# A bidirectional SSD in the gaps of a projection chain: heads in three staggered steps, masks in the exponents, one C B^T for both directions

## The chip, the core and the metric

The kernel runs on one core of one Trainium2 chip. The metric is the device time of one execution in microseconds. The engines are named as in the profile: PE (TensorE, with PEld its weight loads), DVE (VectorE), ACT (ScalarE), POOL (GpSimd), SP (SyncE, which issues most DMAs).

## The reference, cut to what matters

Two blocks of a model of width 2048 are computed in fp32. The first (attention, pooling, a convolutional feed-forward) and the last layer (neighbourhood attention) are not touched. Between them stands the even layer, on 16 meta tokens and 256 tokens (272 columns): projections, then a Mamba-2 SSD in both directions on 32 heads of 64 in 8 groups, a 31-tap convolution branch, and one output projection over both.

```python
z_a, xs, Bm, Cm, dt_f, dt_b, z_b, glu_v, glu_g = split_cols(rmsnorm(h) @ w_in)
xs, Bm, Cm = silu(depthwise_conv5([xs, Bm, Cm]))
# ssd_scan, one direction, chunks of 128:
A_cs = cumsum(log_a);  seg = A_cs[l] - A_cs[s]
Lmat = exp(where(s <= l, seg, -inf))        # per head
Y    = (C B^T * Lmat) @ (x * dt)            # C B^T per group of 4 heads
# y = forward + backward (flipped) + D * x
y_a = rmsnorm(y * silu(z_a))
y_b = silu(layernorm(conv31(glu_v * sigmoid(glu_g)))) * silu(z_b)
h   = h + [y_a, y_b] @ w_out
```

## The kernel before, in words

A projection (`project`) is 48 matmuls of 128x272 into one `acc` tile of PSUM: for each of 16 blocks of the contraction, weights high by input high (L226), high by low (L227) and low by high (L228). The weights arrive as `raw` chunks; ACT copies each half of a chunk to the rounded `wH` (L185), and POOL or DVE subtracts to get `wL` (L186). A table says which: of the chunks of B, C and xs POOL makes both halves, of the chunks of z_a, z_b and glu one, DVE the other. Three `acc` tiles, three `gp` tiles and two `cvp` tiles lie in PSUM.

The even layer goes through its projections in a fixed order: gates and values of the conv branch (glu, from about 1040 us), B and C with their 5-tap convolutions, xs, z_a (1470 to 1605 us), z_b (1608 to 1743 us), then the output projection `e_out`. Everything else is background work: `later(cost, fn)` puts a piece in a queue, and after each projection `run_bg(budget)` takes pieces until their costs reach the budget. The framework then orders the instructions of each engine by itself; engines run in order and wait for one another by semaphores.

The SSD is such background work. `group(g)` makes one C B^T for four heads: two matmuls into `gp` (L837), and a copy for each direction, masked by 0/1 constants, into an 800-wide `cb` (DVE L839, L841, L843, L844; ACT L840). `pair(hp)` treats two heads: transposes of x into `gp` (L866, copied out by L868), a DMA that spreads the cumulated decays over the partitions (`A4`), and per head `head`: five additions of a per-partition bias, limited at `EXP_MAX` (DVE L853), one exponential over 800 columns (ACT L855), one multiply by `cb` (DVE L856), and two additions on POOL that sum the directions where both are in force (L858). In a second step four matmuls with `e` as the weights' partner (L879) and three of the meta part (L885) go into a third `gp` tile, which DVE adds to x (L887). `meta_set` and `meta_x` do the 16 meta columns for eight heads at a time; `meta_x` makes four small copies `dupx` (DVE L820) into two buffers, each followed by a 32-row matmul (L822). In z_a and z_b one pair is done per projection or two.

```python
for a, b in ((144, 0), (672, 400)):
    nc.gpsimd.tensor_tensor(e[:, a:a + P], e[:, a:a + P], e[:, b:b + P], op=OP.add)
...
later(cost, g)
if held:
    later(*held.pop())
```

Of the kernel before, what the change touches and what calls it, by code (L numbers as in the profile page):

```python
# [15 lines left out]
P = 128  # L16
# [3 lines left out]
NM = 16  # L20
# [27 lines left out]
CC = {"mf": (0, 272), "mb": (272, 272), "m0f": (544, 272), "m0b": (816, 16), "bd": (832, 128)}  # L48
# [9 lines left out]
class Kernel:  # L58
# [14 lines left out]
    WIDE = 5  # L73
# [7 lines left out]
    def wide(self, n, name):  # L81
        return self.tp.tile([P, 800], F32, name=name, tag="wide", bufs=self.WIDE)[:, :n]
# [277 lines left out]
    def build(self):  # L360
# [6 lines left out]
        self.ph = lambda name: self.cp.tile([P, 960], F32, name=name, tag="phase", bufs=1)  # L367
# [8 lines left out]
    def load_x(self):  # L376
# [3 lines left out]
        for tag, size, n, steps in (("A4", 1088, 4, (2, 2)), ("A4", 1088, 4, (2, 2)), ("cb", 800, 3, (2, 1)),  # L380
                                    ("cb", 800, 3, (2, 1)), ("wide", 800, 2, (2,))):
# [259 lines left out]
    def even(self):  # L641
# [41 lines left out]
        def time_steps():  # L683
# [45 lines left out]
        for i in range(0, 16, 2):  # L729
            sig = []  # L730
            for j in (i, i + 1):
# [5 lines left out]
                self.run_bg(3.8)  # L737
                self.advance()
            for j in (i, i + 1):
# [5 lines left out]
                self.run_bg(3.8)  # L745
# [29 lines left out]
        for g in range(8):  # L775
            Bs.append(conv5(("B", g), 16 + g))
            self.run_bg(2.4)
            self.advance()
            Cs.append(conv5(("C", g), 24 + g))
            self.run_bg(2.4)  # L780
# [9 lines left out]
        def meta_set(t):  # L790

            a0 = self.wide(N + NM, "a0")
            z = self.wide(N + NM, "z0")
            for h in range(8):
                nc.sync.dma_start(a0[16 * h:16 * h + 16, :N], dA[8 * t + h:8 * t + h + 1].to_broadcast([NM, N]))
                nc.sync.dma_start(a0[16 * h:16 * h + 16, N:],
                                  dA[32 + 8 * t + h:32 + 8 * t + h + 1, :NM].to_broadcast([NM, NM]))
            nc.vector.tensor_scalar(z[:, :N], a0[:, :N], sb0[:, 0, t:t + 1], EXP_MAX, op0=OP.add, op1=OP.min)
            nc.vector.tensor_scalar(z[:, N:], a0[:, N:], sb0[:, 1, t:t + 1], EXP_MAX, op0=OP.add, op1=OP.min)
# [3 lines left out]
            dups = []  # L803
            for d in range(2):
                dup = self.tp.tile([P, 64], F32, name="dup", tag="dup", bufs=2)
                nc.vector.tensor_copy(dup.rearrange("p (a b) -> p a b", a=4),
                                      Bs[2 * t + d][:, :NM][:, None, :].to_broadcast([P, 4, NM]))
                dups.append(dup)
            yield
            ps = self.gp()[:, :N]  # L810
            for d in range(2):
                nc.tensor.matmul(ps[64 * d:64 * d + 64], dups[d], Cs[2 * t + d], start=True, stop=True)
            nc.vector.tensor_tensor(z[:, :N], ps, z[:, :N], op=OP.mult)
            W0[t] = self.split_act(z[:, :N], N)

        def meta_x(t):
            ps = self.gp()[:, :P]
# [5 lines left out]
            x0 = self.work("x0")  # L823
            nc.vector.tensor_tensor(x0[:, :P], ps, cols(cc, CC, "bd"), op=OP.mult)
# [3 lines left out]
            X0[t] = h, l  # L828

        def group(g):  # L830

            cb = self.tp.tile([P, 800], F32, name="cb", tag="cb", bufs=2)
            for c in range(2):
                ps = self.gp()[:, :N]
                nc.tensor.matmul(ps, Bs[g][:, NM + c * P:NM + (c + 1) * P], Cs[g], start=True, stop=True)  # L837
                if c == 0:
                    nc.vector.tensor_tensor(cb[:, :128], ps[:, NM:144], cols(cc, CC, "mb", P + NM, P), op=OP.mult)  # L839
                    nc.scalar.copy(cb[:, 128:144], ps[:, :NM])  # L840
                    nc.vector.tensor_tensor(cb[:, 144:400], ps[:, NM:], cols(cc, CC, "mf", 0, 256), op=OP.mult)  # L841
                else:
                    nc.vector.tensor_tensor(cb[:, 400:528], ps[:, 144:], cols(cc, CC, "mf", 0, P), op=OP.mult)  # L843
                    nc.vector.tensor_tensor(cb[:, 528:], ps, cols(cc, CC, "mb"), op=OP.mult)  # L844
# [407 lines left out]
```

## Time and profile before

| | |
|---|---|
| time, median of 3 runs (lowest to highest) | 2476.81 us (2475.53 to 2478.07) |
| the profiled execution: its own time | 2476.68 us |
| its span | 2474.8 us |
| PE busy | 2419.8 us (98%) |
| DVE busy | 1662.6 us (67%) |
| ACT busy | 1258.8 us (51%) |
| POOL busy | 1093.5 us (44%) |

The shares are means over the whole program. In the rows below, "A <- B" in a wait says whose result A waited for; in a group of instructions "out<-in" names the tiles. PEclk is the granted clock of TensorE, 1.00 being the higher of its two levels (2.4 GHz).

### The profile page before, as it was taken

What the parts mean: (1) busy time and instruction counts of PE and PEld (TensorE: products, weight loads), DVE (VectorE), ACT (ScalarE), POOL (GpSimd) and SP (SyncE); (2) the same over time, 40 slices, a digit from 0 to 9 for tenths busy, and PEclk for the clock granted to TensorE, in tenths of its full rate; (3) what the DMA queues carried; (4) which work ended last, traced back from release to release, by engine and by line L of the source; (5) the groups of instructions that cost most, each with busy time, mean ns of one, the idle gap of its engine ahead of it and who ended that gap; (6) DMA issues with size and microseconds to landing.
All of it is one profiled execution on the core that took longest, in us unless ns stands there. A gap on an engine that the chain in (4) does not pass through costs nothing. (4 is left out here: it accounts for less than half of the span.)

```text
span 2474.8 us, 48425 instructions
## 1 busy us (share of the span) xinstructions
PE 2419.8 (98%) x19742; PEld 2376.2 (96%) x19742; DVE 1662.6 (67%) x2897; ACT 1258.8 (51%) x1917; POOL 1093.5 (44%) x505
## 2 busy tenths in 40 slices
PE   8999999999999999999999998988999999999998
PEld 8998999999999999999999997878999999999998
DVE  6566466667666676889999979888767544444433
ACT  6564555554554554554445564744544444444553
POOL 1134444445445445644367855444334433333443
PEclk9999999999999999999999999999999999999999
DMA  8545655556656656864464554544666544445553
GB/s 283 186 140 190 231 193 186 187 177 219 233 176 216 226 181 215 256 216 174 149 206 169 188 199 140 194 154 153 218 234 207 187 161 164 171 171 171 194 187 120
DMA packets 116415, 471.62 MB, mean 191 GB/s; under 512 B 17376, under 2 KB 54496, under 8 KB 72416
## 3 DMA queue, kind: packets, MB, share of 16 engines
q1 hardware_dynamic: 94880, 443.87, 53.3%
q10 hardware_dynamic: 21312, 24.67, 2.8%
q8 instruction: 154, 2.52, 0.4%
q14 instruction: 69, 0.57, 0.1%
HBM read 448.94 MB, written 19.54 MB: 189 GB/s over the span
## 5 line engine op out<-in xcount | busy, mean ns | idle before, releaser
L226 PE MATMUL acc<-xh,wH 128*128 128x256 f32 (+1 forms) x5856 | 1676.2, 286 | 9.3 <-ACT xh L267 6.3
L228 PE MATMUL acc<-xh,wL 128*128 128x256 f32 (+1 forms) x5856 | 1668.3, 285 | 4.7 <-DVE wL L186 4.4
L227 PE MATMUL acc<-xl,wH 128*128 128x256 f32 (+1 forms) x5856 | 1670.6, 285 | 0.2 <-DVE xl L268 0.2
L186 POOL TENSOR_TENSOR wL<-raw,wH 128x1024 fp32r<-128x1024 f32 (+1 forms) x435 | 1041.0, 2395 | 1305.6 <-ACT wH L185 1187.6
L185 ACT ACTIVATE wH<-raw 128x1024 fp32r<-128x1024 f32 (+1 forms) x838 | 833.2, 998 | 867.2 <-PE acc L227 645.4
L226 PEld LDWEIGHTS acc<-xh,wH 128*128 128x128 f32 x5856 | 1108.8, 189 | 18.4 <-ACT xh L267 6.6
L228 PEld LDWEIGHTS acc<-xh,wL 128*128 128x128 f32 x5856 | 1108.2, 189 | 7.5 <-DVE wL L186 5.5
L227 PEld LDWEIGHTS acc<-xl,wH 128*128 128x128 f32 x5856 | 1108.4, 189 | 1.2 <-DVE xl L268 0.3
L186 DVE TENSOR_TENSOR wL<-raw,wH 128x1024 fp32r<-128x1024 f32 (+2 forms) x403 | 582.1, 1446 | 146.4 <-ACT wH L185 140.8
L666 DVE SCALAR_TENSOR_TENSOR cvp<-u,prm,cvp 128x264 f32<-128x264 f32 (+14 forms) x480 | 210.4, 487 | 0.7 <-ACT cvp L660 0.3
L265 DVE TENSOR_TENSOR xl<-y,xh 128x256 fp32r<-128x256 f32 x44 | 98.7, 2243 | 25.1 <-ACT xh L264 25.1
L239 PE MATMUL acc<-wH,xh 128*128 128x256 f32 x384 | 109.1, 286 | 5.9 <-ACT xh L267 5.9
L590 DVE TENSOR_TENSOR u<-acc,r 128x256 f32<-128x256 f32 x88 | 36.7, 418 | 111.2 <-PE acc L228 109.1
L241 PE MATMUL acc<-wH,xl 128*128 128x256 f32 x384 | 108.9, 285 | 0.7 <-DVE xl L268 0.7
L240 PE MATMUL acc<-wL,xh 128*128 128x256 f32 x384 | 107.7, 283 | 0.0
L239 PEld LDWEIGHTS acc<-wH,xh 128*128 128x128 f32 x384 | 72.9, 191 | 6.2 <-ACT xh L267 6.1
L291 DVE TENSOR_TENSOR nacc<-nacc,sq 128x272 f32<-128x272 f32 (+1 forms) x103 | 70.9, 688 | 9.6 <-ACT sq L280 8.7
L241 PEld LDWEIGHTS acc<-wH,xl 128*128 128x128 f32 x384 | 73.0, 190 | 1.8 <-DVE xl L268 1.4
L858 POOL TENSOR_TENSOR e<-e 128x128 f32<-128x128 f32 x64 | 48.9, 787 | 57.0 <-DVE e L856 56.1
L240 PEld LDWEIGHTS acc<-wL,xh 128*128 128x128 f32 x384 | 72.7, 190 | 0.1
L768 DVE SCALAR_TENSOR_TENSOR gp<-c,prm,gp 128x270 f32<-128x270 f32 (+1 forms) x128 | 63.7, 497 | 7.5 <-ACT gp L764 7.1
L853 DVE TENSOR_SCALAR e<-A,sbT 128x128 f32<-128x128 f32 (+3 forms) x160 | 65.1, 462 | 0.1
(229 smaller groups left out, 1396.5 us busy)
## 6 DMA issues: line engine op xcount, KB each, us to landing
raw<-in_e_w_in_dram SPq DMA_DIRECT2D x97, 1024.0 KB
raw<-in_w_up_dram SPq DMA_DIRECT2D x88, 1024.0 KB
raw<-in_o_w_in_dram SPq DMA_DIRECT2D x64, 1024.0 KB
raw<-in_w_down_dram SPq DMA_DIRECT2D x64, 704.0 KB
raw<-in_e_w_out_dram SPq DMA_DIRECT2D x32, 1024.0 KB
raw<-in_w_qkv_dram SPq DMA_DIRECT2D x21, 1024.0 KB
raw<-in_w_out_dram SPq DMA_DIRECT2D x16, 1024.0 KB
raw<-in_o_w_out_dram SPq DMA_DIRECT2D x16, 1024.0 KB
```

What stands on the lines that cost most here:

```text
L185: nc.scalar.activation(H[:, c], w[:, c], AF.Copy)
L186: eng.tensor_tensor(L[:, c], w[:, c], H[:, c].bitcast(F32), op=OP.subtract)
L226: nc.tensor.matmul(ps, wh, xh, start=k == 0, stop=False)
L227: nc.tensor.matmul(ps, wh, xl, start=False, stop=False)
L228: nc.tensor.matmul(ps, wl, xh, start=False, stop=k == n - 1)
L239: nc.tensor.matmul(ps[b], xh, H[:, o:o + 256], start=k == 0, stop=False)
L240: nc.tensor.matmul(ps[b], xh, L[:, o:o + 256], start=False, stop=False)
L241: nc.tensor.matmul(ps[b], xl, H[:, o:o + 256], start=False, stop=k == 15)
L265: nc.vector.tensor_tensor(l, x, h.bitcast(F32), op=OP.subtract)
L291: nc.vector.tensor_tensor(st["acc"], st["acc"], sq, op=OP.add)
L666: nc.vector.scalar_tensor_tensor(cps[i][:, a:b], u[i][:, a + s:b + s], self.prm_("dww", k * 16 + i), cps[i][:, a:b], op0=OP.mult, op1=OP.add)
L853: nc.vector.tensor_scalar(e[:, o:o + n], A4[:, d, i, l:l + n], sbT[:, c, 32 * d + h:32 * d + h + 1], EXP_MAX, op0=OP.add, op1=OP.min)
```

## The change

A pair becomes three steps, queued one projection slot apart: the transposes and the DMA of `A4`; the exponentials and their products (`heads`); the matmuls and the addition to x. The step of one pair is queued beside the other steps of its neighbours.

In `heads` the bias goes into the exponential itself: per head seven ACTIVATEs of 16 to 144 columns with the bias as a per-partition operand. The limit `EXP_MAX` is gone there; instead `cum` is held above -2^29, and on the triangular squares `A4` is held, by a minimum with constants of plus or minus 1e30 (`sq`), at or below -1e30 where the mask is zero. So the mask comes out of the exponential as zero. The squares of the backward direction go to a tile `eb`, DVE adds them (L865), and one multiply of 544 columns by a `cb` without masks (L866 of the new kernel) serves both directions. `group` is two plain copies on ACT. The result `py` goes into `cvp` instead of `gp`. `meta_set` takes in `meta_x`: the DMAs a step early, the copies `dup` and `dupx` into the tail of `z0` in the step before the matmuls, and one 128-column matmul for four. The tile `wide` shrinks from 800 to 544 columns, with seven buffers for five. The budgets are 3.4 for 3.8 (glu), 2.9 for 2.4 (B, C, xs), 3.9 for 4 (z_a, z_b); the pieces `yb` of z_b are split from the ninth z_b on, and the remaining queue is emptied beside the output projection with a budget of 3.9.

```diff
-                self.run_bg(3.8)
+                self.run_bg(3.4)
...
+            nc.vector.tensor_scalar(cum, cum, -2.0 ** 29, None, op0=OP.max)
...
-            self.run_bg(2.4)
+            self.run_bg(2.9)
...
+            dup = zt[:, 288:416].rearrange("p (d a b) -> p d a b", d=2, a=4)
+            for d in range(2):
+                nc.vector.tensor_copy(dup[:, d], Bs[2 * t + d][:, :NM][:, None, :].to_broadcast([P, 4, NM]))
+            dupx = zt[:, 416:].rearrange("p (i a b) -> p i a b", i=4, a=2)
+            for i in range(4):
+                nc.vector.tensor_copy(dupx[:, i], xs[4 * t + i][:, :NM][:, None, :].to_broadcast([P, 2, NM]))
...
+            yield
+            px = self.gp()[:, :P]
+            nc.tensor.matmul(px, zt[:, 416:], self.ident, start=True, stop=True)
...
-            for i in range(4):
-                dup = self.tp.tile([P, 32], F32, name="dupx", tag="dupx", bufs=2)
-                nc.vector.tensor_copy(dup.rearrange("p (a b) -> p a b", a=2),
-                                      xs[4 * t + i][:, :NM][:, None, :].to_broadcast([P, 2, NM]))
-                nc.tensor.matmul(ps[32 * i:32 * i + 32], dup, self.ident, start=True, stop=True)
...
-                if c == 0:
-                    nc.vector.tensor_tensor(cb[:, :128], ps[:, NM:144], cols(cc, CC, "mb", P + NM, P), op=OP.mult)
...
+                nc.scalar.copy(cb[:, N * (1 - c):N * (2 - c)], ps)
...
-            nc.scalar.activation(e, e, AF.Exp)
-            nc.vector.tensor_tensor(e, e, cb, op=OP.mult)
-            for a, b in ((144, 0), (672, 400)):
-                nc.gpsimd.tensor_tensor(e[:, a:a + P], e[:, a:a + P], e[:, b:b + P], op=OP.add)
...
+            def exp(to, i, d, c, l, n):
+                h = 32 * d + 2 * hp + i
+                nc.scalar.activation(to, A4[:, d, i, l:l + n], AF.Exp, bias=sbT[:, c, h:h + 1])
+
+            for i in range(2):
+                exp(E[i][:, 416:544], i, 0, 0, 144, P)
+                exp(E[i][:, 272:288], i, 1, 0, 0, NM)
+                exp(E[i][:, 0:144], i, 1, 1, 0, 144)
+            for d in range(2):
+                sq = A4[:, d, :, NM:].rearrange("p i (c l) -> p i c l", c=2)
+                nc.vector.tensor_tensor(sq, sq, cols(cc, CC, "sq", P * d, P)[:, None, None, :]
+                                        .to_broadcast([P, 2, 2, P]), op=OP.min)
+            for i in range(2):
+                for c in range(2):
+                    o = 288 - 144 * c
+                    exp(E[i][:, o:o + P], i, 0, c, NM + P * c, P)
+                    exp(B[i][:, 1 - c], i, 1, c, NM + P * c, P)
+            for e, eb in zip(E, B):
+                nc.vector.tensor_tensor(squares(e), squares(e), eb, op=OP.add)
+                nc.vector.tensor_tensor(e, e, CBF[hp // 2], op=OP.mult)
...
-            py = self.gp()[:, :N]
+            yield
+            E = heads(hp, A4)
+            yield
+            py = self.cvp()
...
+        for s in range(18):
+            if s >= 2:
+                later(1.0, pairs[s - 2])
+            if s % 4 == 1 and s < 16:
+                later(1.8, metas[s // 4])
+            if s < 16:
+                if s % 2 == 0:
+                    self.later(1.0, group, s // 2)
+                later(0.6, pairs[s])
+            if 1 <= s < 17:
+                later(3.6, pairs[s - 1])
...
+            self.run_bg(3.9)
+            if i >= 8:
+                ready(i - 8)
...
-            self.run_bg(1e9)
+            self.run_bg(3.9)
```

On PE, between the second and the third projection of z_b, stand the matmuls of one pair, a group's C B^T and the transposes of a later pair (the numbers tell tiles apart). Before:

```order
L879 MATMUL gp_19933<-e_19747,xt_19742 64x272
L879 MATMUL gp_19933<-e_19757,xt_19742 64x272
L879 MATMUL gp_19933<-e_19747,xt_19742 64x272
L879 MATMUL gp_19933<-e_19757,xt_19742 64x272
L885 MATMUL gp_19933<-xh_19836,x0_19660 128x272
L885 MATMUL gp_19933<-xl_19837,x0_19660 128x272
L885 MATMUL gp_19933<-xh_19836,x0_19661 128x272
L837 MATMUL gp_19943<-c5_16513,c5_16438 128x272
L837 MATMUL gp_19948<-c5_16513,c5_16438 128x272
L866 MATMUL gp_19952<-cst_73,c5_17652 128x128 x2
```

and now:

```order
L888 MATMUL cvp_19840<-e_19751,xt_19627 64x272
L888 MATMUL cvp_19840<-e_19752,xt_19627 64x272
L888 MATMUL cvp_19840<-e_19751,xt_19627 64x272
L888 MATMUL cvp_19840<-e_19752,xt_19627 64x272
L894 MATMUL cvp_19840<-xh_19739,x0_19735 128x272
L894 MATMUL cvp_19840<-xl_19740,x0_19735 128x272
L894 MATMUL cvp_19840<-xh_19739,x0_19736 128x272
L833 MATMUL gp_19850<-c5_16507,c5_16430 128x272
L833 MATMUL gp_19853<-c5_16507,c5_16430 128x272
L879 MATMUL gp_19859<-cst_73,c5_17674 128x128 x2
```

The pair's seven matmuls move from the pool of three `gp` tiles to `cvp`; four tiles of `gp` follow one another before, three now.

On ACT, about the same place. Before, from one copy of weights to the next tanh but one:

```order
L185 ACTIVATE wH_19986<-raw_19868 128x1024
L947 ACTIVATE tanh_19928<-z_b_19927 128x272
L840 COPY cb_19942<-gp_19943 128x16
L868 COPY xt_19955<-gp_19952 128x256
L855 ACTIVATE e_19970<-e_19970 128x800
L185 ACTIVATE wH_20084<-raw_19980 128x1024
L855 ACTIVATE e_20062<-e_20062 128x800
L185 ACTIVATE wH_20088<-raw_19980 128x1024
L947 ACTIVATE tanh_20040<-z_b_20039 128x272
```

and now, from a copy of weights to the next:

```order
L185 ACTIVATE wH_19894<-raw_19775 128x1024
L965 ACTIVATE tanh_19835<-z_b_19834 128x272
L849 ACTIVATE e_19988<-A4_19856,sbT_13204 128x128
L849 ACTIVATE e_19988<-A4_19856,sbT_13204 128x16
L834 COPY cb_19849<-gp_19850 128x272
L849 ACTIVATE e_19988<-A4_19856,sbT_13204 128x144
L834 COPY cb_19849<-gp_19853 128x272
L881 COPY xt_19862<-gp_19859 128x256
L849 ACTIVATE e_20176<-A4_19979,sbT_13204 128x128
L849 ACTIVATE e_20177<-A4_19979,sbT_13204 128x128
L849 ACTIVATE e_19987<-A4_19856,sbT_13204 128x128 x2
L849 ACTIVATE e_19988<-A4_19856,sbT_13204 128x128
L849 ACTIVATE eb_19989<-A4_19856,sbT_13204 128x128 x2
L185 ACTIVATE wH_20013<-raw_19888 128x1024
```

One exponential of 800 columns per head has become seven short ones, which read `A4` and no longer a tile that DVE has written, and the copies of C B^T are ACT's, 272 columns each.

On DVE, the copies of the second half of x's meta columns for the first eight heads. Before, behind the fourth z_a:

```order
L937 TENSOR_TENSOR z_a_18354<-acc_18305,r_13269 128x272
L820 COPY dupx_18365<-c5_17045 128x32
L820 COPY dupx_18368<-c5_17120 128x32
L839 TENSOR_TENSOR cb_18377<-gp_18378,cc_13200 128x128
L186 TENSOR_TENSOR wL_18422<-raw_18295,wH_18421 128x1024
L824 TENSOR_TENSOR x0_18371<-gp_18358,cc_13200 128x128
L841 TENSOR_TENSOR cb_18377<-gp_18378,cc_13200 128x256
```

and now, for the second eight heads, in the convolutions of the last xs (L770 is a tap of these):

```order
L801 TENSOR_SCALAR z0_18613<-z0_18613,sb0_13205 128x272
L770 SCALAR_TENSOR_TENSOR gp_17899<-c5_17897,prm_72,gp_17899 128x271
L802 TENSOR_SCALAR z0_18613<-z0_18613,sb0_13205 128x16
L770 SCALAR_TENSOR_TENSOR gp_17899<-c5_17897,prm_72,gp_17899 128x270
L806 COPY z0_18613<-c5_15958 128x64
L806 COPY z0_18613<-c5_16112 128x64
L809 COPY z0_18613<-c5_17206 128x32
L809 COPY z0_18613<-c5_17283 128x32
L809 COPY z0_18613<-c5_17360 128x32
L809 COPY z0_18613<-c5_17443 128x32
L764 TENSOR_TENSOR c5_17974<-acc_17925,r_13269 128x272
L186 TENSOR_TENSOR wL_17997<-raw_17915,wH_17996 128x1024
```

The copies stood right ahead of their matmuls; now all six of a set stand in a step before, with other work behind them.

## Rows read from the trace of the kernel before

**Rows 1.** The page's first line: the span.

```profile
span 2474.8 us, 48425 instructions
```

**Rows 2.** Windows; columns: stretch, its length, busy us (instructions) by engine, PEclk, DMA, GB/s.

```profile
1800.00:1900.00 100.00, 100.00 (x802) 99.92 (x801) 67.82 (x92) 46.30 (x65) 39.58 (x16) 1.00 0.67 220
1200.00:1300.00 100.00, 95.60 (x755) 94.45 (x754) 96.96 (x203) 46.73 (x58) 53.49 (x22) 1.00 0.52 174
1300.00:1400.00 100.00, 100.00 (x800) 99.79 (x799) 92.75 (x219) 57.27 (x81) 79.58 (x34) 1.00 0.52 178
1465.00:1745.00 280.00, 255.52 (x1842) 229.96 (x1841) 234.79 (x448) 153.01 (x227) 131.78 (x97) 0.95 0.51 166
1612.00:1711.00 99.00, 85.90 (x607) 75.29 (x607) 91.50 (x178) 46.45 (x74) 43.68 (x42) 0.93 0.49 154
1490.00:1500.00 10.00, 5.31 (x26) 4.18 (x27) 7.62 (x18) 2.56 (x8) 4.44 (x1) 0.66 0.57 206
1570.00:1580.00 10.00, 7.64 (x28) 5.05 (x27) 7.62 (x19) 9.93 (x15) 6.35 (x5) 0.67 0.45 153
1680.00:1690.00 10.00, 5.29 (x26) 5.29 (x27) 9.72 (x27) 4.91 (x8) 3.15 (x5) 0.66 0.56 181
```

**Rows 3.** Waits of PE, 1465 to 1745 us; columns: total us, times, longest.

```profile
PE gp L866 <- DVE c L887: 11.6, 2, 6.5
PE gp L822 <- DVE dupx L820: 5.4, 1, 5.4
PE gp L879 <- POOL e L858: 3.9, 2, 2.4
PE gp L885 <- DVE xl L265: 3.2, 1, 3.2
```

**Rows 4.** Waits of PE, 1200 to 1300 us.

```profile
PE acc L228 <- DVE wL L186: 4.4, 4, 1.7
```

**Rows 5.** The tile view of z_b, its first line.

```profile
L946 DVE SCALAR_TENSOR_TENSOR z_b<-acc,r x16: 422/429/442, 1612.3 to 1741.7; 128x272 f32<-128x272 f32 x16
```

**Rows 6.** Waits of the other engines, 1465 to 1745 us.

```profile
POOL e L858 <- DVE e L856: 56.1, 18, 6.8
...
ACT e L855 <- DVE e L853: 24.1, 8, 6.2
```

**Rows 7.** DVE by line and shape, 1465 to 1745 us.

```profile
L186 DVE TENSOR_TENSOR wL<-raw,wH 128x1024 fp32r<-128x1024 f32 x33 | 47.8, 1449 | 8.0 <-ACT wH L185 7.8
L856 DVE TENSOR_TENSOR e<-e,cb 128x800 f32<-128x800 f32 x32 | 36.8, 1170 | 3.1 <-ACT e L855 3.1
```

**Rows 8.** The page's costliest groups, whole span.

```profile
L666 DVE SCALAR_TENSOR_TENSOR cvp<-u,prm,cvp 128x264 f32<-128x264 f32 (+14 forms) x480 | 210.4, 487 | 0.7 <-ACT cvp L660 0.3
...
L858 POOL TENSOR_TENSOR e<-e 128x128 f32<-128x128 f32 x64 | 48.9, 787 | 57.0 <-DVE e L856 56.1
...
L853 DVE TENSOR_SCALAR e<-A,sbT 128x128 f32<-128x128 f32 (+3 forms) x160 | 65.1, 462 | 0.1
```

**Rows 9.** ACT by line and shape, 1612 to 1711 us.

```profile
L855 ACT ACTIVATE e<-e 128x800 f32<-128x800 f32 x15 | 13.0, 867 | 20.8 <-DVE e L853 20.8
...
L855 ACT ACT_TABLE_LOAD x1 | 1.3, 1283 | 1.5 <-DVE e L853 1.5
...
L868 ACT COPY xt<-gp 128x256 f32<-128x256 f32 x8 | 2.9, 364 | 3.2 <-PE gp L866 3.2
...
L826 ACT ACTIVATE x<-x 128x128 fp32r<-128x128 f32 x1 | 0.3, 310 | 3.7 <-DVE x L824 3.7
```

**Rows 10.** POOL by line and shape, 1760 to 1820 us.

```profile
L186 POOL TENSOR_TENSOR wL<-raw,wH 128x1024 fp32r<-128x1024 f32 x11 | 26.4, 2402 | 40.8 <-ACT wH L185 28.1 <-PE acc L227 12.7
```

**Rows 11.** DVE by line and shape, 1760 to 1820 us.

```profile
L291 DVE TENSOR_TENSOR nacc<-nacc,sq 128x272 f32<-128x272 f32 x11 | 26.7, 2428 | 8.7 <-ACT sq L280 8.7
```

**Rows 12.** ACT by line and shape, 100 to 200 us.

```profile
L475 ACT ACTIVATE s<-s,mx 128x128 f32<-128x128 f32 x8 | 3.2, 403 | 8.7 <-DVE mx L473 5.7 <-DVE win L514 2.9
```

**Rows 13.** PE by line and shape, 1465 to 1745 us.

```profile
L822 PE MATMUL gp<-cst,dupx 128*32 128x128 f32 x32 | 4.2, 302 | 5.4 <-DVE dupx L820 5.4
```

More of the change, by code (lines that the diff above doesn't have):

```diff
@@ L81, in wide @@
     def wide(self, n, name):
-        return self.tp.tile([P, 800], F32, name=name, tag="wide", bufs=self.WIDE)[:, :n]
+        return self.tp.tile([P, 544], F32, name=name, tag="wide", bufs=self.WIDE)[:, :n]
     def small(self, n, name):
@@ L828, in meta_x @@
             X0[t] = h, l
+            W0[t] = self.split_act(z[:, :N], N)
         def group(g):
-            cb = self.tp.tile([P, 800], F32, name="cb", tag="cb", bufs=2)
-            for c in range(2):
+            cb = self.tp.tile([P, 800], F32, name="cb", tag="cb", bufs=2)[:, :2 * N]
+            for c in (1, 0):
                 ps = self.gp()[:, :N]
                 nc.tensor.matmul(ps, Bs[g][:, NM + c * P:NM + (c + 1) * P], Cs[g], start=True, stop=True)
-                if c == 0:
-                    nc.vector.tensor_tensor(cb[:, :128], ps[:, NM:144], cols(cc, CC, "mb", P + NM, P), op=OP.mult)
[L840 to L844, printed above, removed]
@@ new lines, in group, with squares, heads @@
+            CBF[g] = cb
+        def squares(t):
+            return t[:, 144:432].rearrange("p (c n) -> p c n", n=144)[:, :, :P]
+        def heads(hp, A4):
+            E = [self.wide(544, "e") for i in range(2)]
+            B = [self.tp.tile([P, 2, P], F32, name="eb", tag="eb", bufs=2) for i in range(2)]
+            def exp(to, i, d, c, l, n):
[17 more added lines that the diff above has]
+                nc.vector.tensor_tensor(e, e, CBF[hp // 2], op=OP.mult)
+            return E
@@ L863, in pair @@
             x = xs[hp]
+            A4 = self.tp.tile([P, 2, 2, N], F32, name="A4", tag="A4", bufs=2)
+            for d in range(2):
+                nc.sync.dma_start(A4[:, d].rearrange("p a b -> p (a b)"),
+                                  dA[32 * d + 2 * hp:32 * d + 2 * hp + 2].rearrange("a b -> (a b)")[None, :]
+                                  .to_broadcast([P, 2 * N]))
             px = self.gp()
@@ L868, in pair @@
             nc.scalar.copy(xt, px[:, :256])
-            A4 = self.tp.tile([P, 2, 2, N], F32, name="A4", tag="A4", bufs=2)
-            for d in range(2):
-                nc.sync.dma_start(A4[:, d].rearrange("p a b -> p (a b)"),
-                                  dA[32 * d + 2 * hp:32 * d + 2 * hp + 2].rearrange("a b -> (a b)")[None, :]
-                                  .to_broadcast([P, 2 * N]))
-            E = [head(2 * hp, A4), head(2 * hp + 1, A4)]
             yield
-            py = self.gp()[:, :N]
+            E = heads(hp, A4)
+            yield
+            py = self.cvp()
             for c in range(2):
@@ L911, in even @@
         later = lambda cost, g: self.later(cost, next, g, None)
-        held = []
         cn = conformer_norm()
-        norms = [(2.8, cn)] * 4 + [(1.8, cn)] * 4
-        def start(cost, g, rest):
-            later(cost, g)
-            if held:
-                later(*held.pop())
-            held.append((rest, g))
-            if norms:
-                later(*norms.pop(0))
-        for t in range(4):
-            start(2.5, meta_set(t), 0.4)
-            self.later(1.0, meta_x, t)
-            for g in (2 * t, 2 * t + 1):
-                self.later(2.0, group, g)
-                for hp in (2 * g, 2 * g + 1):
-                    start(4.0, pair(hp), 0.5)
-        later(*held.pop())
+        norms = [2.8] * 4 + [1.8] * 4
+        pairs, metas = [pair(hp) for hp in range(16)], [meta_set(t) for t in range(4)]
+        later(0.1, metas[0])
+        later(3.4, metas[0])
+        for s in range(18):
[9 more added lines that the diff above has]
+                later(3.6, pairs[s - 1])
+            if s % 4 == 2 and s < 14:
+                later(0.1, metas[s // 4 + 1])
+            if s % 4 == 3 and s < 15:
+                later(3.4, metas[s // 4 + 1])
+            if norms:
+                later(norms.pop(0), cn)
         gates = []
@@ L949, in even @@
             nc.vector.scalar_tensor_tensor(conv[i], th, 1.0, conv[i], op0=OP.add, op1=OP.mult)
[L950 removed]
+            self.run_bg(3.9)
+            if i >= 8:
+                ready(i - 8)
         del X, self.X
[L952 to L955 removed]
+        for i in range(8, 16):
+            ready(i)
         st = self.norm_begin(N)
```

76 lines of the change are left out of this document (29 added, 47 removed).

## The prediction

> **What bounds the kernel now.** I take the sum against the profiled execution: 2476.7 us, of which 2474.8 is the span [rows 1]; the median of the runs shown is 2476.8, so one figure serves for both. I first read windows. From 1800 to 1900 us PE is never idle and does 802 matmuls in 100 us [rows 2]: 0.1247 us each, 5.99 for a projection of 48. That is the floor, and most of the program sits on it. Two stretches that the change touches don't: 1200 to 1300 (end of glu), where PE lacks 4.4 of 100 while DVE is busy for 97, and 1465 to 1745 (z_a and z_b), where PE lacks 24.5 of 280 and its clock is 0.95 [rows 2]. The convolutions between them keep PE busy all the time (1300 to 1400 us [rows 2]), so nothing is to be won there.
>
> Next the waits of PE. In z_a and z_b four causes carry it [rows 3]: transposes L866 wait for a free `gp` tile, because DVE's L887 has not yet emptied the one of the pair before (11.6 us in two waits); one 32-row matmul waits for its small copy (5.4); the pair's own matmuls wait for POOL's additions (3.9); the meta part waits for a rounded piece `xl` (3.2). 0.4 more falls on L837. In glu all 4.4 is PE waiting for `wL` of DVE [rows 4]. So DVE is late both times.
>
> Then z_b slot by slot. Its sixteen projections end in 129.4 us [rows 5]; the last five have no heads beside them and take 5.99 each, which leaves 99.4 for ten, 9.9 per slot. The window of those ten slots, 1612 to 1711, shows DVE busy for 91.5 of 99 us, ACT for 46.5, POOL for 43.7 [rows 2]. POOL waits 56.1 us for DVE's multiply, and ACT 24.1 us for DVE's additions [rows 6]: DVE is at the head of that chain. PE was busy for 85.9 there; without the two clock dips in it (below) that is 82.3, or 8.2 per slot. **The slot of 9.9 is DVE's, and the next limit is PE's own 8.2.**
>
> **What DVE loses and gets.** Per pair before: two multiplies of 1.17 [rows 7], ten additions with a limit, 65.1/16 = 4.07 [rows 8], and half of a group's four masked copies, up to 272 columns each, for which DVE's reading of `acc` in z_b shows 0.43 [rows 5], so up to 0.8. Together 7.2. After: per pair two minima of 512 columns, two additions of 256, two multiplies of 544. No row shows these widths; between 272 columns at 0.43 [rows 5] and 800 at 1.17 [rows 7] a straight line gives 0.77, 0.41 and 0.81, sum of the six 4.0. (The 1.17 contains blocked time, so the line is rather high.) So 3.2 less per pair. The window of ten slots holds the transposes of eight pairs [rows 9], 0.8 per slot, and DVE's 9.15 becomes 9.15 - 2.6 = 6.6. POOL loses its 64 additions, 48.9 us [rows 8].
>
> Two-input operations can be held up by POOL. While POOL split weights at 2.40 us each [rows 10], the 272-column addition L291 took 2.43 [rows 11], against 0.43 for the operation of that width that reads PSUM [rows 5]: 2.0 us lost to one split. In a slot with one split of POOL that makes 6.6 to 8.6 for DVE. The Trainium skill, "SBUF — State Buffer", section "Who interferes with whom", says that DVE and GpSimd share one port pair as an exclusive lock, and that a DVE instruction with two SBUF inputs fully blocks against a GpSimd instruction that reads SBUF. The trace agrees (2.43 beside 2.40), and the rule speaks against this change, since all six new operations have two SBUF inputs. If each slot lost a whole split, the slots would come to 8.6 on DVE, still below 9.9.
>
> **What ACT gets.** Per pair, minus two exponentials of 0.87 [rows 9]; plus twelve of 128 to 144 columns, between 0.31 (a copy of 128 columns with no bias [rows 9]) and 0.40 (an exponential of 128 with a per-partition bias [rows 12]), 3.7 to 4.8; plus two of 16 columns, 0.3; plus half of two copies of C B^T at about 0.37 each (L868, 256 columns, 0.36 [rows 9]). Net +2.7 to +3.8. ACT's 4.65 per slot becomes 7.4 to 8.5 where a whole pair falls in it. That is close to PE's 8.2.
>
> A new hand-over comes with it: the minimum overwrites `A4`, so DVE waits until ACT's first exponentials have read it, and ACT's other eight wait for the minimum. Behind the waiting DVE instruction stand the evictions of `acc` and `wL`; behind ACT's stand `wH` and the copies that free `gp`; PE waits for all of these. The order puts a weight copy or the other head between the two halves, so I price it at 0 to 1.0 per pair.
>
> **The terms.**
> (1) Glu. In the order, the taps from the time-step projection to the end of glu fall from 112 to 103, and one `wL` goes from DVE to POOL: about 9 times 0.44 (210.4/480 [rows 8]) and 1.45 [rows 7], 5.4 off DVE, more than the 4.4 it is late. -4.4 (0 to -4.4). The taps move on into the convolutions, but the budget of 2.9 changes little there: the order has about 8 taps per projection before and after, because it was the scheduler that decided.
> (2) Waits in z. The 5.4 go: the copies stand a step early, covered by convolution taps. The 12.0 on `gp` go: the pair's result is in `cvp`, which the convolutions have left, and `gp` is emptied by ACT. What is late next is ACT's copies behind up to 4.8 us of exponentials, hidden by the projection between; if that cover is gone, the 12 come back as waits for ACT. The 3.9 go with POOL's additions, since the products are queued a slot ahead of the matmuls. The 3.2 for `xl` stay; the first set is as tight as before. -21.3 (0 to -24.5).
> (3) Clock. Four windows of 10 us at 0.66 or 0.67, so part of each at the lower level, each with a wait that goes in it or just before: the first, the second and the last have 5.31, 7.64 and 5.29 us of busy PE [rows 2] and lose 1.8, 2.5 and 1.8, and the third, around 1635 us, is like the last. -8 (0 to -9.5 with small dips).
> (4) Twelve matmuls of 32 rows fewer: three quarters of 4.2 us [rows 13], less what overlaps. -2.5 (0 to -3.1).
> (5) New limit. PE's 8.2 per slot is met by ACT's 7.4 to 8.5 and DVE's 6.6 to 8.6 with a hand-over. Were none in the way it costs 0; with ACT at 8.5 plus a whole hand-over the slot is 9.5, +1.3 in each of 16, +21. I take 8.65, near the upper ends of both engines: +0.45 times 16, **+7**.
>
> At nothing: the DMAs of `A4` and `z0` a step earlier (same count; on SP they stand ahead of weight loads, and no wait of PE on a weight's DMA is in [rows 3]; DMA share 0.49 in z_b [rows 2]); the smaller `wide`, seven for five; the clamp of `cum`, one operation; the split of `yb` in z_b, which the order had there before; the budget beside the output projection, since the queue is empty by then in both orders.
>
> Sum: -4.4 - 21.3 - 8 - 2.5 + 7 = -29.2, so **2447.5 us**.
>
> **The rivals.**
> (A) ScalarE becomes the pace, and it gets slower. Exponentials, the tanh of z_b's gate and the square roots of norms are spread over ACT's order; if each pair slot saw two switches of its tables at 1.28 [rows 9], it would need 8.5 + 2.6 = 11.1 us. Then waits of PE for ACT replace all the old ones: 16 times 1.2 = +19, less terms 1 and 4, so about 2489. It decides from 9.9 + 6.9/16 = 10.3 us per slot. For it: the order has 51 table loads in the program, 43 before. Against it: in z_a and z_b they fall from 17 to 12, and the extra ones lie in the convolutions, where PE runs ahead. The Trainium skill, "ScalarE: Activation LUTs", section "What ACT_TABLE_LOAD costs", gives about 2.66 us per switch, the load and a drain. By that estimate two switches would be 5.3 us, and the slot 13.8. The trace shows the load's 1283 ns, and no run here shows a drain behind it. Chance 0.10.
> (B) DVE stays the pace: six two-input operations meet POOL's splits more than once per slot, 6.6 + 2.0 and more, and the hand-over keeps it at 9.9. Only glu and the fewer matmuls remain: 2470. For it speaks that DVE's multiplies take 1.17 [rows 7], already partly blocked; against it, that POOL's additions, which hold the same ports, are gone. Chance 0.12, half of it within 0.2%.
> (C) Half of the waits go: ACT now empties `gp` from behind its exponentials, or the matmuls wait for the products. -4.4 - 10.6 - 4 - 2.5 + 7 = -14.5, about 2462. Chance 0.16.
> The forecast itself, 2434 to 2456, has 0.62.
>
> **How the numbers follow.** 2447.5 is the likeliest case. The range of 2434 to 2470 goes from all waits and dips gone with no new limit (-40, and a little for dips between the windows) to (B); it leaves out (A) and the slow half of (B). A measurement here tells about 0.2%, 5 us, from no change. Faster by that: 0.62 + 0.16 + half of (B) = 0.84; the same: 0.06; slower: 0.10.
>
> **What would show it.** PE waits in z_a and z_b below 8 us instead of 24.5, none for L866 on L887 or for `dupx`; clock above 0.98 there; ten busy slots of z_b at 8.5 to 8.9; DVE below 85% and ACT above 75% busy in them; no wait for `wL` around 1240 us; no POOL addition of `e`. Wrong if PE waits for ACT's copies or exponentials (A, C), if DVE's new operations average well over 1 us (B), or if a wait appears in the convolutions, where three pairs' exponentials now start.

## The result, and the profile after

The changed kernel takes 2449.3 us (2448.7 to 2449.7, four runs) against 2477.1 us before: ratio 0.9889, 95% interval 0.9877 to 0.9901, 28 us less. The forecast was 2447.5. Its profiled execution took 2449.6 us.

Windows of the kernel after; columns as in [rows 2]. First the ten slots of z_b with heads, then z_a and z_b as a whole, the end of glu, and five windows with a lower clock:

```profile
1602.00:1683.00 81.00, 79.27 (x583) 70.75 (x582) 73.23 (x119) 57.88 (x149) 22.62 (x9) 0.98 0.50 166
1465.00:1717.00 252.00, 241.10 (x1784) 221.08 (x1783) 210.16 (x318) 178.87 (x391) 84.05 (x32) 0.97 0.54 182
1200.00:1300.00 100.00, 99.97 (x799) 99.75 (x798) 99.58 (x206) 48.48 (x62) 54.67 (x23) 1.00 0.53 183
1470.00:1480.00 10.00, 4.43 (x25) 3.04 (x24) 8.49 (x12) 5.00 (x9) 2.56 (x1) 0.93 0.55 194
1480.00:1490.00 10.00, 10.00 (x75) 10.00 (x75) 8.47 (x19) 4.94 (x11) 2.40 (x1) 0.90 0.42 149
1550.00:1560.00 10.00, 6.80 (x38) 5.16 (x37) 10.00 (x20) 5.05 (x10) 3.33 (x2) 0.85 0.27 75
1560.00:1570.00 10.00, 10.00 (x67) 9.88 (x66) 4.64 (x6) 7.70 (x15) 2.42 (x1) 0.81 0.48 182
1640.00:1650.00 10.00, 9.15 (x58) 8.44 (x60) 9.90 (x15) 5.75 (x15) 2.84 (x1) 0.83 0.46 163
```

The first line of its tile view of z_b, which answers to [rows 5]:

```profile
L964 DVE SCALAR_TENSOR_TENSOR z_b<-acc,r x16: 426/432/442, 1602.2 to 1713.4; 128x272 f32<-128x272 f32 x16
```

Its waits of PE from 1465 to 1717 us, which answer to [rows 3]:

```profile
PE gp L817 <- DVE mu L905: 4.4, 1, 4.4
PE cvp L894 <- DVE xl L265: 4.0, 3, 3.2
PE gp L879 <- ACT c L773: 1.2, 1, 1.2
PE gp L814 <- ACT cb L834: 1.2, 1, 1.2
```

The reader sees that glu is full, that the three waits of [rows 3] which were to go have gone (L866 for DVE's addition, the copies, POOL's additions), that the one for `xl` stayed, and that a new one of 4.4 us came: a meta matmul waits for a `gp` tile that holds the sum of the convolution branch until DVE reads it. The wait for `xl` has the old name but another place: before, it stood ahead of the first pair's meta matmuls (about 1512 us); now these wait 0.4 us, and the 3.2 stand at the fifth pair's (about 1554 us), where the second set of meta columns begins. z_b takes 111.2 us instead of 129.4; less five slots of 5.99, its ten busy slots take 8.1 each instead of 9.9. That is a little too good, since the first eviction of z_b now begins 2.3 us after PE has begun the next projection (0.4 before): counted by the starts of PE's projections the ten slots take 8.3 each instead of 10.0.

A second count places the gain without any model of waits: the start of the first, the 2600th, 3500th, 4100th and last of the 5856 matmuls of L226, read from each trace (us between them).

```
                 to 2600  to 3500  to 4100  to the end
before             940.7    344.1    311.5    707.9
after              941.0    338.6    288.3    709.1
```

Of the 27.0 us in the profiles 5.5 lie in glu and the convolutions, 23.2 in z_a and z_b (6.3 of them in z_a, 17.0 in z_b), and 1.2 are given back later: 0.8 of it in the next 16 projections, beside the output projection, whose budget the change also sets (6.05 each instead of 5.99). Why they are slower was not looked into.

### The profile page after: what moved, and what is told of

Read it like the earlier page. It is cut to its first block, busy times and chain, and to the rows that moved or that the text cites. A ratio compares the mean times of both kernels' runs of the same rounds, so it can differ in the third digit from the quotient of the medians.

```text
span 2447.8 us, 48352 instructions
## 1 busy us (share of the span) xinstructions
PE 2410.7 (98%) x19718; PEld 2373.6 (97%) x19718; DVE 1639.5 (67%) x2770; ACT 1308.1 (53%) x2125; POOL 1046.8 (43%) x441
## 4 chain that ended last, share of the span: by engine, by line
PE 90%; DVE 3%; issue 2%; ACT 2%; DMA 1%; SPq 0%; POOL 0%; ACTq 0%; POOLq 0%; DVEq 0%
PE acc L226 27%; PE acc L227 27%; PE acc L228 27%; PE acc L241 2%; PE acc L239 2%; PE acc L240 2%; ACT wH L185 1%; PE cvp L1078 1%; PE gp L1068 1%; DVE wL L186 1%; DVE win L513 1%; PE gp L1044 1%; PE cvp L888 0%; DVE e L865 0%; ACT e L849 0%
## 5 line engine op out<-in xcount | busy, mean ns | idle before, releaser
L226 PE MATMUL acc<-xh,wH 128*128 128x256 f32 (+1 forms) x5856 | 1675.1, 286 | 9.4 <-ACT xh L267 6.2
L226 PEld LDWEIGHTS acc<-xh,wH 128*128 128x128 f32 x5856 | 1108.5, 189 | 17.6 <-ACT xh L267 6.6
L241 PEld LDWEIGHTS acc<-wH,xl 128*128 128x128 f32 x384 | 73.2, 191 | 1.6 <-DVE xl L268 1.5
L770 DVE SCALAR_TENSOR_TENSOR gp<-c,prm,gp 128x270 f32<-128x270 f32 (+1 forms) x128 | 63.8, 498 | 5.7 <-ACT gp L766 5.3
L622 DVE TENSOR_TENSOR xw<-acc,xw 128x256 f32<-128x256 f32 x64 | 27.2, 425 | 51.6 <-PE acc L228 48.2
L592 ACT ACTIVATE y<-u,prm 128x256 f32<-128x256 f32 x88 | 52.2, 594 | 14.9 <-DVE u L590 14.7
```

The lines of the kernel that those rows point to most:

```text
L226: nc.tensor.matmul(ps, wh, xh, start=k == 0, stop=False)
L241: nc.tensor.matmul(ps[b], xl, H[:, o:o + 256], start=False, stop=k == 15)
L770: nc.vector.scalar_tensor_tensor(y[:, a:b], t[:, a + d:b + d], self.prm_("ecw", k * 32 + c), y[:, a:b], op0=OP.mult, op1=OP.add)
```

## The experiments

Twelve kernels in three sets of four; all times of a set stand beside runs of the kernel before on the same chip. The changed kernel was not run again in these sets, so a comparison with its 2449.3 is one across chips. "Stretch" is the time from the 3500th to the 4100th matmul as above (before 311.5, after 288.3).

**1. The pair's result in `gp` again.**

```diff
-            py = self.cvp()
+            py = self.gp()[:, :N]
```

> The changed kernel, but the pair's result goes into a gp tile again, so that four gp tiles follow one another in a slot with a group, on three buffers. Theory (place: the two long waits of L866 came from the shared pool, whatever DVE's load): most of the 12 us of waits for gp come back and with them 2 to 4 us of clock, 2449 + 8 to 16 = 2457 to 2465, with waits of PE for the addition to x (L896) in the trace. Rival (load: the waits came from DVE being late, and DVE has 2.6 us less per slot now): the tiles come free in time, within 3 us of the changed kernel's 2449.

2457.0 us, ratio 0.9917 (0.9903 to 0.9932), stretch 299.5. Two of its PE waits, 1465 to 1730 us:

```profile
PE gp L879 <- ACT cb L834: 5.4, 2, 3.7
PE gp L879 <- DVE c L896: 4.4, 3, 2.4
```

9.8 us of waits for `gp` come back, in front of the same transposes; 5.4 of them are now for a tile that ACT empties. The place counts, also with DVE relieved.

**2. That edit alone, on the kernel before.**

```diff
-            py = self.gp()[:, :N]
+            py = self.cvp()
```

> The kernel before, with this alone changed: the pair's result goes into cvp. Theory (place): the 11.6 us of L866 and the clock dips behind them go, -10 to -15, about 2464. Rival (load: DVE paces the slots of 9.9 us, and the wait only shows up elsewhere): the waits move to other instructions (the pair's matmuls on e, acc on wL), and the time falls by less than 4 us.

2485.8 us, ratio 1.0033 (1.0021 to 1.0045), stretch 322.3: slower. All its PE waits, 1465 to 1760 us:

```profile
PE cvp L879 <- POOL e L858: 14.9, 6, 5.1
PE gp L822 <- DVE dupx L820: 5.9, 2, 5.4
PE cvp L879 <- DVE c L887: 3.3, 1, 3.3
PE cvp L885 <- DVE xl L265: 3.0, 1, 3.0
```

The waits of L866 are gone, and the pair's matmuls wait 14.9 us for the products instead of 3.9 [rows 3]. Both theories missed the size, but the rival's mechanism is what the rows show: while DVE is late, a free tile lets PE run into the next thing that DVE owes. The waits alone don't make the loss: they come to 27.1 us for 24.5, and the stretch is 10.8 longer. The rest is clock. By windows of 10 us, busy time of PE times what the granted clock lacks is 17.6 us here and 9.5 before. So `cvp` is worth 7.7 us with the new heads (8.8 against number 4, on the same chip) and costs 9 without them.

**3. The budgets alone, on the kernel before** (3.4 for 3.8 in glu, 2.9 for 2.4 in the convolutions).

> The kernel before, with the budgets of the changed one alone (3.4 in glu, 2.9 in B, C and xs). Theory: the 4.4 us of PE waiting for wL in glu go and nothing else, -4.4, about 2472.7. Rival (the earlier start of the heads' work, which the larger budget in the convolutions brings, is worth something by itself): more than 8 us less. Second rival: the budgets shift nothing that counts, because the scheduler orders the taps: within 1.5 us of before.

2471.3 us, ratio 0.9974 (0.9964 to 0.9984). From 1200 to 1300 us two PE waits are left, 1.0 us in all for 4.4 [rows 4]:

```profile
PE acc L228 <- POOL wL L186: 0.8, 1, 0.8
PE acc L228 <- DVE wL L186: 0.2, 1, 0.2
```

The stretch keeps 310.8, so the earlier start of the heads is worth next to nothing by itself; of the gain of 5.7, 4.3 lie between the 2600th and the 3500th matmul, in glu and the convolutions. The first theory holds, a little larger.

**4. The meta copies written in the step of their matmuls.**

```diff
             nc.scalar.activation(z, z, AF.Exp)
-            dup = zt[:, 288:416].rearrange("p (d a b) -> p d a b", d=2, a=4)
...
             yield
+            dup = zt[:, 288:416].rearrange("p (d a b) -> p d a b", d=2, a=4)
...
             px = self.gp()[:, :P]
```

> The changed kernel, but the copies dup and dupx of the meta columns stand in the step of their matmuls again (still one 128-column matmul, with a buffer of their own). Theory (the wait of 5.4 us came from copies that queue on DVE right ahead of their matmuls): one to three waits of L814 or L817 on the copies, 2 to 6 us slower, 2451 to 2455. Rival (it came from the two buffers that the four copies took in turn, L820 waiting for L822): no such wait, within 1 us of 2449.

2448.2 us, ratio 0.9882 (0.9866 to 0.9899), no wait for a copy. In DVE's order the copies stand at the same places as before the edit, but for four of the third set, which stand a few instructions later: the framework lifts them. So it is not the step in which they are written. The cause of the 5.4 us stays open. The trace of the kernel before shows this much:

```profile
1487.99 0.41 PE L822 MATMUL gp<-cst,dupx 128*32 128x128 f32 x4
1492.67 2.05 DVE L820 COPY dupx<-c 128x32 f32<-128x32 f32 x2
```

The matmuls that read the first two copies were over at 1488.4 us, and so the two buffers were free; the third copy began 4.3 us later, behind other work in DVE's order. What PE waited for was the copy's place in that order. Whether the two buffers put it there no run shows, as none had the old buffers in the new kernel; that one matmul now stands for four is a rival that was not separated either.

**5 to 8. Removing single waits of the new kernel.** The sum of the convolution branch in `cvp`; the last meta step a slot earlier; both; and the norm's later pieces every other step:

```diff
-            ps = self.sum_finish(lsum)
+            ps = self.cvp()[:, :N]
+            nc.tensor.matmul(ps, self.ones, lsum["acc"], start=True, stop=True)
...
-            if s % 4 == 1 and s < 16:
+            if s % 4 == 0 and s < 16:
                 later(1.8, metas[s // 4])
...
-            if norms:
+            if norms and (s < 4 or s % 2 == 1):
                 later(norms.pop(0), cn)
```

> The changed kernel, but the sum of the convolution branch's mean goes into a cvp tile instead of gp. In the changed kernel's trace one wait is new: the meta matmul L817 waits 4.4 us for gp until DVE's L905 has read that sum, late behind three multiplies L866 that take 4.1 us. Theory (the wait is for the tile of gp alone): it goes, and with it 1 to 2 us of clock behind it, 2449.3 - 5 to 6 = 2443.5. Rival (DVE is late there whatever the tile): PE waits for something else of DVE at that place, within 1.5 us of 2449.

> The changed kernel, but the last step of the meta columns (their matmuls and the split into x0, W0) is queued one projection slot earlier. Theory (the wait of 3.2 us for xl before L894 comes from a split made in the same slot in which it is used): it goes, with the 2 to 3 us of clock behind it, about 2444. Rival (the earlier step meets the same busy DVE and only waits elsewhere, L817 on gp among them): within 2 us of 2449.

> Both of the two edits above. Theory: they add up, 2449.3 - 11 = 2438 to 2440, with less than 4 us of PE waits left between z_a's start and z_b's end. Rival: each removes the same late moment of DVE, and both give no more than the better one, about 2444.

> The changed kernel, with the pieces of the convolution branch's norm after the fourth queued in every other step instead of every one. In the changed kernel the split xl of the second meta set stands on DVE behind 14 multiplies L914 (several held up by POOL's splits), and PE waits 3.2 us for it, with two clock dips behind. In the new order xl stands ahead of L914. Theory (order on DVE at that place): the 3.2 and 2 to 3 us of clock go, ratio 0.9889 - 0.0024 = 0.9865. Rival (DVE is late there as a whole, as the three edits before showed: the wait moves to the next thing that PE needs of DVE): within 0.0008 of 0.9885.

2449.8, 2449.5, 2449.2 and 2449.5 us (ratios 0.9878, 0.9878, 0.9874 and 0.9892, each interval 0.0029 to 0.0033 wide): none differs measurably from the changed kernel. Each wait that was aimed at went, and about as much came elsewhere. The first row of PE waits of the first (sum in `cvp`), 1465 to 1717 us:

```profile
PE cvp L894 <- DVE xl L265: 8.6, 3, 5.0
```

the longest of the second (meta step earlier), in the same stretch:

```profile
PE cvp L894 <- DVE xl L265: 4.2, 1, 4.2
PE gp L833 <- ACT cb L834: 3.8, 1, 3.8
PE gp L833 <- DVE z L821: 2.7, 1, 2.7
```

and of the last (norm spread):

```profile
PE gp L817 <- DVE mu L905: 4.3, 1, 4.3
PE cvp L888 <- DVE e L866: 3.6, 2, 3.1
PE gp L879 <- DVE m L307: 1.8, 1, 1.8
```

With the rows not shown the sums are 11.0, 11.3 and 12.2, against 10.8 of the changed kernel. In the first, the first pair's meta matmul, which now comes up earlier, waits 5.0 us. In the second, the wait of 3.2 at the fifth pair went, and the same name came back at the first pair with 4.2. The rivals of the single edits were right three times; of the two together neither the 2438 to 2440 nor the 2444 came. The name in a row of waits is only the first thing that PE asks of a late engine. That this engine is DVE is what most rows say (3.8 us in the second are for a copy of ACT), and it fits number 9.

**9. The additions of the squares on POOL.**

```diff
-                nc.vector.tensor_tensor(squares(e), squares(e), eb, op=OP.add)
+                nc.gpsimd.tensor_tensor(squares(e), squares(e), eb, op=OP.add)
```

> The changed kernel, with the additions of the two directions' squares on POOL as before (32 of 256 columns instead of 64 of 128). Theory (DVE's relief and POOL's absence from the pair's chain both count): POOL's additions wait behind splits of 2.6 us, DVE's multiply behind them, and some of that reaches PE: 3 to 8 us slower, 2452 to 2457. Rival (DVE gains 16 times 2 us and a hand-over is hidden by the projection between): within 2 us, or faster.

2444.7 us, ratio 0.9863 (0.9848 to 0.9878): 5 us faster than the kernels 5 to 7 on the same chip, so the rival holds, and the forecast loss does not come. The stretch is 285.3, 3.0 less than in the changed kernel. (It is from the profiled execution, which took 2449.9 us; the other three took 2443.9 to 2444.9. Up to the 2600th matmul the profiled one took 945.0 us for 941.0 in the changed kernel, and the edit touches nothing there.) Its window of 1602 to 1683 us has DVE busy for 63.5 of 81 us instead of 73.2:

```profile
1602.00:1683.00 81.00, 77.33 (x561) 68.30 (x561) 63.48 (x103) 56.81 (x147) 35.56 (x23) 0.98 0.52 166
```

and its PE waits, 1465 to 1717 us, have one long entry left:

```profile
PE cvp L894 <- DVE xl L265: 7.0, 3, 6.2
PE cvp L894 <- ACT xh L264: 1.7, 1, 1.7
```

**10. That, with the norm spread.**

> The same edit, with the additions of the squares on POOL. The version with these additions on POOL alone had a ratio of 0.9863 and still one wait of 6.2 us for the same xl, behind nine multiplies that took 7.3 us. Theory (DVE's load and the order at that place both count): the wait goes, -6 to -9 us with its clock, ratio 0.983 to 0.984, the fastest of all. Rival: the wait moves, ratio 0.986 as without the edit.

2442.9 us (2442.6 to 2443.6), ratio 0.9865 (0.9850 to 0.9880), stretch 281.9; the norm's spread alone took 2449.5 (2449.0 to 2450.1) on the same chip, so the additions bring 6.6 here. The ratio is the rival's, not the 0.983 to 0.984 of the theory. But by the rows the wait for `xl` does not move on to other work of DVE any more. All PE waits, 1465 to 1717 us:

```profile
PE cvp L894 <- ACT xh L264: 3.7, 2, 2.3
PE cvp L888 <- DVE e L866: 0.7, 1, 0.7
PE cvp L894 <- DVE xl L265: 0.4, 1, 0.4
PE gp L879 <- DVE m L307: 0.4, 1, 0.4
```

5.2 us instead of 10.8, and 3.7 of it for a copy of ACT. The lowest time of all, below both kernels; whether the spread adds to number 9 the ratios of two chips don't tell.

**11. A pair in two steps again** (transposes, `A4`, exponentials and products in one step, the matmuls in the next).

> The changed kernel with a pair in two steps again: transposes, the DMA of A4, exponentials and products in one step, the matmuls one projection slot later (the last meta step stands ahead of the first pair's matmuls of its slot). Theory (the products stand a slot ahead of their matmuls in either form, and A4's DMA lands long before it is needed, so the third step gives little): within 3 us of the changed kernel, ratio 0.988 to 0.990. Rival (the stagger carries the gain: the exponentials wait for A4, and the matmuls for the exponentials): waits of PE for e and of ACT for the DMA of A4, 8 us slower or more, ratio above 0.992.

2453.6 us, ratio 0.9909 (0.9894 to 0.9923), stretch 295.2: 4 us slower, between the two. Its long PE waits, 1465 to 1725 us, are neither for the products nor for `A4`:

```profile
PE cvp L893 <- ACT xh L264: 6.3, 2, 3.4
PE cvp L893 <- DVE xl L265: 3.8, 2, 3.4
PE cvp L893 <- ACT x L823: 2.6, 1, 2.6
```

The stretch is 6.9 us longer than in the changed kernel; the waits are 12.9 us for 10.8, and the clock (counted as in number 2) costs 10.6 for 5.8. In ACT's order the splits of the meta part now stand behind a whole pair's exponentials, at 1555 us behind three table loads too; which of these makes them late is not separated. The edit also moved the last meta step ahead of a pair's matmuls, so it doesn't separate the stagger from that.

**12. Two table changes in each busy slot.**

```diff
-            nc.scalar.activation(th, t, AF.Tanh)
+            nc.scalar.activation(th, t, AF.Sigmoid)
```

> The changed kernel with the tanh of z_b's gate replaced by a sigmoid (this changes what z_b's gate computes), so that ACT must change its table before the gate and again before the exponentials, in the slots of z_b that have both: some 14 table loads more in the order, 18 us of ACT. The window of z_b's ten busy slots has ACT busy for about 80% now. Rival A of the prediction: ACT has no room for two loads of 1.28 in a slot, and z_b's ten slots grow by 1.0 to 2.4 us each, 10 to 20 us slower, ratio 0.993 to 0.997. Theory (ACT has slack of about 1.5 us per slot, and PE runs ahead of it by a projection): less than 5 us slower, ratio below 0.991.

2459.8 us, ratio 0.9933 (0.9918 to 0.9947), stretch 298.4: 10 us slower, rival A's price at its lower end. Table loads on ACT, 1465 to 1750 us, by the line behind them, two of six groups (after the change alone 7 for L849 and none for L965; 33 in all instead of 15):

```profile
L849 ACT ACT_TABLE_LOAD x15 | 19.2, 1283 | 0.9 <-DVE z_a L949 0.8
...
L965 ACT ACT_TABLE_LOAD x10 | 12.8, 1283 | 0.2
```

and the PE wait that came with them:

```profile
PE cvp L888 <- DVE e L866: 7.5, 6, 1.8
```

18 loads of 1.28 add 23 us to ACT, of which 10 reach PE: spread over ten slots, 1.0 where ACT gets 2.3 more. The difference of 1.3 is near the slack of 1.5 that the theory had; its bound of 5 us didn't follow from that, as 2.3 less 1.5 in ten slots is already 8. Its other premise was wrong: ACT is busy for 71% of the ten slots in the changed kernel (57.9 of 81 us), not for about 80%.

## Why the prediction was right, and where its parts were not

The time (2449.3 for 2447.5) is right, and so is the mechanism that carried it: DVE set the slots of z_b, and with its work cut PE comes near its own limit. No run gave DVE its old work back alone; that its load counts is shown by number 9, which cuts it further, and by numbers 1 and 2, where one edit has opposite signs with and without the relief. That the sum fits within 2 us is in part luck, since its errors cancel: the clock gave 4.3 less than counted, and glu 1.1 and a rest of 3.4 more. Of the signs named in advance, four came (no wait for L887's tile or for `dupx`, none for `wL`, no addition of `e` on POOL) and five missed: PE waits of 10.8 us (forecast: below 8), a clock of 0.97 (above 0.98), slots of 8.1 to 8.3 (8.5 to 8.9), DVE busy for 90% (below 85), ACT for 71% (above 75). By the terms:

**(1) Glu, -4.4.** Right: no wait is left, the stretch to the 3500th matmul loses 5.5, and the budgets alone (number 3) bring 5.7.

**(2) Waits in z, -21.3.** The listed ones went by that much (11.6, 0.4, 5.4 and 3.9 to nothing) and `xl` went from 3.2 to 4.0. But "the first set is as tight as before" is wrong: its wait fell to 0.4, and the second set's came. That "the copies stand a step early" is not why the 5.4 went either (number 4). What the term lacks is that two of the edits in it only pay together: with DVE late, `cvp` costs 9 us (number 2); with `gp`, the new heads lose 7.7 (number 1).

**(3) Clock, -8.** Too large. The five windows above lose 0.3, 1.0, 1.0, 1.9 and 1.6 us (busy PE times what the clock lacks), 5.8 in all, against 9.5 before: -3.7. The new wait of 4.4, the one for `xl` at the fifth pair and one of 1.2 (L814) each have a dip behind them.

**(4) Fewer matmuls, -2.5.** Thirty-two records of 4.2 us [rows 13] became eight of 1.8 (L814): -2.4.

**(5) New limit, +7.** The size is right by luck. It was to be a pace of 8.65 per busy slot set by ACT and DVE; the slots take 8.1 to 8.3, near PE's own 8.2, as ACT's load stayed far below the 8.5 of the term (below). What came instead are 6.8 us of new waits, 4.4 of them at one place in z_a. There DVE does three multiplies in 4.1 us, ahead of the operation that reads the sum. The timeline of POOL and DVE:

```profile
1473.85 2.56 POOL L186 TENSOR_TENSOR wL<-raw,wH 128x1024 fp32r<-128x1024 f32 x1 [4.39 <-ACT wH L185]
1473.49 4.14 DVE L866 TENSOR_TENSOR e<-e,cb 128x544 f32<-128x544 f32 x3
1477.55 0.43 DVE L949 TENSOR_TENSOR z_a<-acc,r 128x272 f32<-128x272 f32 x1
1477.90 0.42 DVE L905 TENSOR_SCALAR mu<-gp 128x272 f32<-128x272 f32 x1
```

The second of the three took 2.87 us for 0.72 of the others: it began while POOL's split ran and ended after it.

With the terms as measured z comes to -21.3 + 0.8 + 6.8 - 3.7 - 2.4 = -19.8 against 23.2 counted; 3.4 us stay without a row. They are in PE's busy time, as its waits are all counted.

**DVE's share: the single operations right, their meetings with POOL too few.** Its three new groups, 1465 to 1717 us (the columns as in [rows 7]):

```profile
L865 DVE TENSOR_TENSOR e<-e,eb 128x256 f32<-128x256 f32 x29 | 29.6, 1027 | 15.1 <-ACT eb L849 15.0
L857 DVE TENSOR_TENSOR A<-A,cc 128x512 f32<-128x512 f32 x28 | 27.5, 1004 | 10.9 <-ACT e L849 10.9
L866 DVE TENSOR_TENSOR e<-e,cb 128x544 f32<-128x544 f32 x32 | 26.8, 856 | 2.7 <-ACT cb L834 2.2
```

I had 0.41, 0.77 and 0.81: 4.0 per pair. They take 1.03, 1.00 and 0.86, 5.8 per pair, so of 7.2 only 1.4 went, and DVE is busy for 90% of the ten slots (forecast: below 85%). The addition of 256 columns takes longer than the multiply of 544: most of it is waiting. The timeline shows for what. An addition alone, and one that begins while POOL splits weights:

```profile
1571.03 0.43 DVE L865 TENSOR_TENSOR e<-e,eb 128x256 f32<-128x256 f32 x1 [0.29 <-ACT eb L849]
1662.52 2.40 POOL L186 TENSOR_TENSOR wL<-raw,wH 128x1024 fp32r<-128x1024 f32 x1 [6.96 <-ACT wH L185]
1663.07 2.14 DVE L865 TENSOR_TENSOR e<-e,eb 128x256 f32<-128x256 f32 x1 [1.34 <-ACT eb L849]
```

Of the 29 additions, 18 began while no split ran and took 0.41 to 0.43 us; 11 began during one, took 1.53 to 2.59, and each ended 0.28 us after the split did. The minima take 0.68 and the multiplies 0.72 where they are not held; five and two of them were held in the same way, for 2.2 to 2.9 us in all. (Two minima at 1516.5 us ran through during a split, which itself took 4.2.) So the straight line was right, even a little high, and what the forecast had too low is how often DVE meets a split: 18 of these 89 operations were held. The Trainium skill, "SBUF — State Buffer", section "Who interferes with whom", calls the port pair of the two engines an exclusive lock, which a DVE operation with two inputs from SBUF contends for; the trace agrees (2.02 us on average during a split, 0.42 otherwise).

**ACT: the single operations were forecast well, the sum was not.** The exponentials, same stretch:

```profile
L849 ACT ACTIVATE e<-A,sbT 128x128 f32<-128x128 f32 x83 | 31.0, 391 | 6.8 <-DVE A L857 4.2 <-DVE z_a L949 1.5 <-DVE m L307 1.0
L849 ACT ACTIVATE eb<-A,sbT 128x128 f32<-128x128 f32 x57 | 21.1, 390 | 2.6 <-DVE A L857 1.7 <-DVE z_a L949 0.9
L849 ACT ACTIVATE e<-A,sbT 128x144 f32<-128x144 f32 x27 | 10.9, 405 | 2.2 <-DVE z_a L949 2.2
...
L849 ACT ACTIVATE e<-A,sbT 128x16 f32<-128x16 f32 x27 | 8.0, 295 | 0.0
```

0.39 to 0.41, the upper end of the range, and 0.30 for the narrow ones (I had 0.15). But ACT is busy for only 57.9 us of the ten slots, 5.8 per slot where the forecast had 7.4 to 8.5. The forecast's figure is for a slot with a whole pair, and the ten slots hold the exponentials of about 6.8 pairs. Also, lengths can't be added up, since operations that follow at once overlap:

```profile
1663.23 0.39 ACT L849 ACTIVATE eb<-A,sbT 128x128 f32<-128x128 f32 x1
1663.52 0.39 ACT L849 ACTIVATE e<-A,sbT 128x128 f32<-128x128 f32 x1
```

Each takes 0.39, and they start 0.29 apart. The hand-over by the minimum costs ACT 5.9 us of waiting (4.2 and 1.7) in the whole stretch, a third of a microsecond per pair.

**Rival A** was no phantom: with two table changes per slot the gain shrinks by 10 us (number 12), though not below zero as I had it. It was priced from 8.5 us of ACT per slot; with 5.8 and 2.3 of loads ACT needs 8.1, not 11.1. The Trainium skill, "ScalarE: Activation LUTs", section "What ACT_TABLE_LOAD costs", adds a drain of 1.38 us to each load. In number 12 a load starts at 1649.13 us, 0.01 after the copy ahead of it ends, and its exponential at 1650.42, 1.29 later; so no run shows a drain on either side.

## What to carry to other kernels

A row of waits names the thing that PE asked for, not why its maker was late: four edits that each removed the named wait changed nothing, and moving one addition per head off the late engine brought 5 us. So first ask how busy the releasing engine is over the whole stretch and what holds its operations up (here POOL's splits), and only then for buffers and order. Two edits can have opposite signs alone and together (`cvp`: +9 without the relief of DVE, -7.7 with it); measure them in both settings before one is dropped.

## What the runs showed of the hardware that I had not expected

The additions of two directions are cheaper for the kernel on POOL, though POOL takes 0.87 us for 256 columns where DVE alone takes 0.43: on DVE the mean was 1.03. A DVE addition that began during a POOL split ended 0.28 us after it, eleven times of eleven. A load of ACT's table costs the kernel about 0.56 us here (10 us for 18 loads), less than half its length; ACT was busy for 71% of the ten slots before the loads came.
